# Gates by Strassen's seven products after all branch projections, and w_out opened by three token tiles

## The chip, the cores and the metric

The kernel runs on one core of one Trainium2 chip, in one launch. Its time is the device time of that core in microseconds, median of the runs given. The engines: PE (TensorE: matmuls and transposes, with PEld for its weight loads), ACT (ScalarE), DVE (VectorE), POOL (GpSimd), and SP, whose queue issues most DMAs. Each engine works through its own instructions in the order of its stream; semaphores let it wait for another engine or for a DMA. PE's results go to PSUM, which has eight banks of 128 x 512 fp32 here: two for transposes ("tr"), four for products in turn ("mm"), two for sums ("acc").

## What is computed

One layer of a hybrid decoder: two attention branches (FoX and NSA), merged by gates, an output projection, and an MLP with squared ReLU. The tokens are 512 of a prompt and 64 of samples (8 sequences of 8), D = 1024. The part that is changed is the merge and what follows it:

```python
def post_mixer(x, pm, o_fox, o_nsa, lp):
    br_fox = jnp.einsum('btk,kd->btd', o_fox.reshape(b, t_len, FOX_QW), lp['w_br_fox'])
    br_nsa = jnp.einsum('btk,kd->btd', o_nsa.reshape(b, t_len, NSA_QW), lp['w_br_nsa'])
    mix = pm['g_fox'] * br_fox + pm['g_nsa'] * br_nsa
    x = x + pm['gt1'] * jnp.einsum('btd,de->bte', mix, lp['w_out'])
    h = rms_norm(x, lp['norm2_g']) * (1.0 + pm['sc2']) + pm['sh2']
    u = jax.nn.relu(jnp.einsum('btd,df->btf', h, lp['w_up']))
    return x + pm['gt2'] * jnp.einsum('btf,fd->btd', u * u, lp['w_down'])
```

The gates g_fox and g_nsa are sigmoids of 1024 columns each of h @ w_in, where h is the normalized input. Each branch projection has 512 inputs and 1024 outputs.

## The kernel before

**fp32 by three products.** A value is split into a high part, rounded by a copy on ACT (L112, to the type fp32r), and a low part, the difference, formed on DVE (L131). A product of two such pairs is three matmuls: high by high, low by high, high by low. Names end in h or H, l or L for the parts. The tokens are worked in two halves of HALF = 288 columns, so one product of 128 output features, 1024 inputs and one half is 8 x 3 = 24 matmuls of 128 x 288.

**The mix** (`mix_part`, L1873 on) works by tiles e = 0 to 7 of 128 output features, called tiles of the mix here. For each tile and each of the two gates x it runs the gate's product (names mg, weights wm from w_in, 2 halves x 24 = 48 matmuls) and then the branch's projection (names br, weights wb, 512 inputs, 2 x 12 = 24 matmuls). ACT forms the tanh of half the gate's product out of PSUM, two instructions per gate. DVE forms (t + 1) times the branch out of PSUM (L109), which gives twice the gated branch; the factor of two is taken out later. GpSimd adds the two gated branches (L1944), and `split_pack` writes the high and low part of the sum to `mix2`, in the order that w_out's matmuls read. Tile 0 is special: its first gate is started earlier (`mix_first`), and its two branches come after both gates. The raw weights go through `praw`, a pool of three buffers of 512 KB each, filled by SP's queue.

**w_out** (`out_part`, L1980) works by token tiles i, five of them (0 to 3 of the prompt, 4 with the samples), in the order 0, 4, 1, 2, 3, and for each by q = 0 to 3: q % 2 is the half of the inputs, q // 2 the half of the 1024 outputs. So (i, q) is 12 matmuls of 128 x 512 for tile 0 to 3, 8 for tile 4. Each q has a weight of its own, wo0 to wo3. After an odd q, DVE multiplies by the gate (`wot`) and adds to x (`x2` in the code; all of x is loaded early). A finished tile is normalized: ACT sums its squares, DVE makes the reciprocal root in small steps and scales the rows (`nsq`), and PE transposes them (names nt) to give h3, the input of the MLP. Where these transposes stand is set by hand:

```python
        rest, turn_at = {}, {(1, 1): 0, (2, 0): 4, (2, 3): 1}
```

This reads: ahead of the matmuls of (1, 1) come the transposes of tile 0, ahead of (2, 0) those of tile 4, ahead of (2, 3) those of tile 1; those of tile 2 come after the last matmul. `self.chain` fixes the order of PE in this stage to that of the code; the other engines' order comes from a scheduler that places instructions by its own model.

**up** (`mlp_up`) is the MLP's first projection. Most of its tiles are already formed by Strassen's seven products, from pairs of feature tiles and the two halves of tokens and inputs, by `product`, with sums of the weights made on DVE at first and on GpSimd later (L2116).

## Time and profile before

| | us |
|---|---|
| median of 3 runs | 1194.47 |
| lowest and highest run | 1192.92, 1195.43 |
| the profiled run, by the clock of the runs | 1193.61 |
| its span in the profile | 1191.8 |

The span is the time from the first to the last instruction of the profiled execution. All positions in the text are microseconds from its start. In a row of the timeline the numbers are the start and the duration; then come the engine, the line, the operation, out<-in, and in brackets the idle time ahead of it and what ended it. In a group there stand the count, the busy time, the mean of one in ns, and the idle time ahead.

### The profile page before, as it was taken

To read this page: it belongs to the slowest core of one execution; us is meant where nothing else is said; L and a number is where in the kernel's file an instruction comes from. 1 tells how busy PE (TensorE), PEld (TensorE's weight loads), DVE (VectorE), ACT (ScalarE), POOL (GpSimd) and SP (SyncE) were. 2 spreads that over 40 slices of the span, in tenths; PEclk is the share of its full clock that TensorE was granted. 3 is DMA by queue.
4 is the path that set the end of the run, shared out by engine and by line. 5 is a ranking of instruction groups with operands and counts; after the bars stand their busy time and mean duration, and the time that the engine had idled before them with its cause. 6 is when DMAs were issued, how large, how long until landed. Compare 5 with 4: busy or idle time off the path is not lost.

```text
span 1191.8 us, 24394 instructions
## 1 busy us (share of the span) xinstructions
PE 1149.2 (96%) x9111; PEld 986.7 (83%) x9111; DVE 767.8 (64%) x1968; ACT 558.7 (47%) x1185; POOL 159.6 (13%) x174
## 2 busy tenths in 40 slices
PE   3899999999999999999999999999999999999998
PEld 3887789999666656777799999789999997888886
DVE  3588785586788866666643434668767844554586
ACT  2455463353777864555532223356556656222230
POOL 2012100000321130000300000002565400000000
PEclk9999999999999989999999999999999999999999
DMA  9599555796685457999963333355534535445312
GB/s 211 158 248 260 168 147 194 248 321 225 189 287 175 136 165 248 324 298 308 230 171 85 79 95 122 103 176 180 162 133 163 186 133 191 153 173 166 111 28 80
DMA packets 166840, 215.35 MB, mean 181 GB/s; under 512 B 18329, under 2 KB 136546, under 8 KB 164546
## 3 DMA queue, kind: packets, MB, share of 16 engines
q1 hardware_dynamic: 145602, 174.21, 47.5%
q0 software_dynamic: 9280, 25.16, 6.8%
q10 hardware_dynamic: 11840, 14.42, 3.9%
q8 instruction: 72, 1.18, 0.4%
q14 instruction: 46, 0.38, 0.1%
HBM read 190.11 MB, written 44.53 MB: 197 GB/s over the span
## 4 chain that ended last, share of the span: by engine, by line
PE 81%; DVE 6%; DMA 5%; ACT 3%; SPq 3%; issue 2%; ACTq 0%; DVEq 0%
PE dn L77 17%; PE mg L77 9%; PE z L77 6%; PE hid L77 5%; PE br L77 4%; PE wo L77 4%; PE up L77 3%; SPq L162 3%; PE ss L77 3%; PE so L77 2%; PE k L83 2%; PE ct L83 2%; DMA cpg<-in_cache_nsa_kv 2%; PE ada L77 1%; PE sp L83 1%
## 5 line engine op out<-in xcount | busy, mean ns | idle before, releaser
L77 PE MATMUL z<-winh,h 128*128 128x264 f32 (+1 forms) x576 | 111.0, 286 | 0.3
L77 PEld LDWEIGHTS z<-winh,h 128*128 128x128 f32 x576 | 91.7, 190 | 2.1 <-DVE h L794 0.9
L77 PE MATMUL z<-winl,h 128*128 128x264 f32 (+1 forms) x320 | 88.2, 284 | 0.5 <-DVE winl L131 0.5
L112 ACT ACTIVATE xh<-ct 128x256 fp32r<-128x256 f32 x128 | 48.0, 384 | 61.6 <-PE ct L83 36.0
L77 PE MATMUL mg<-hH,wml 128*128 128x288 f32 x256 | 75.4, 296 | 0.9 <-DVE wml L131 0.9
L77 PE MATMUL mg<-hH,wmh 128*128 128x288 f32 x256 | 75.4, 296 | 0.0
L100 DVE TENSOR_TENSOR acc<-acc,dn 128x512 f32<-128x512 f32 x60 | 41.0, 684 | 51.0 <-PE dn L77 50.9
L77 PE MATMUL mg<-hL,wmh 128*128 128x288 f32 x256 | 72.6, 294 | 0.0
L131 DVE TENSOR_TENSOR xl<-ct,xh 128x256 fp32r<-128x256 f32 x128 | 51.6, 420 | 16.0 <-ACT xh L112 14.2
L77 PEld LDWEIGHTS z<-winl,h 128*128 128x128 f32 x320 | 60.6, 190 | 0.7 <-DVE winl L131 0.7
L83 PE MATMUL ct<-identF,ro 128*128 128x128 f32 x256 | 36.5, 283 | 23.0 <-DVE ro L115 22.8
L131 DVE TENSOR_TENSOR wml<-wmr,wmh 128x1024 fp32r<-128x1024 f32 x14 | 17.1, 1225 | 56.4 <-ACT wmh L112 56.4
L83 PEld LDWEIGHTS ct<-identF,ro 128*128 128x128 f32 x256 | 30.2, 147 | 25.8 <-DVE ro L115 18.5
L77 PEld LDWEIGHTS mg<-hH,wml 128*128 128x128 f32 x256 | 48.1, 188 | 1.1 <-DVE wml L131 1.1
L77 PEld LDWEIGHTS mg<-hH,wmh 128*128 128x128 f32 x256 | 48.1, 188 | 0.2
L77 PEld LDWEIGHTS mg<-hL,wmh 128*128 128x128 f32 x256 | 47.2, 188 | 0.1
L77 PE MATMUL hid<-xh,w1hlv 128*128 128x512 f32 (+1 forms) x160 | 44.7, 365 | 0.7 <-ACT xh L112 0.5
L77 PE MATMUL hid<-xh,w1hlk 128*128 128x512 f32 (+1 forms) x160 | 44.6, 367 | 0.1
L131 DVE TENSOR_TENSOR wp<-sums,wp 128x1024 fp32r<-128x1024 f32 x26 | 38.0, 1468 | 9.2 <-ACT wp L112 8.5
L112 ACT ACTIVATE mgt<-mg 128x288 f32<-128x288 f32 x32 | 12.9, 410 | 59.1 <-PE mg L77 59.1
L131 DVE TENSOR_TENSOR wp<-pu,wp 128x512 fp32r<-128x512 f32 (+1 forms) x26 | 30.2, 1167 | 14.7 <-ACT wp L112 14.7
L77 PE MATMUL br<-oH,wbh 128*128 128x288 f32 x128 | 37.8, 296 | 0.2 <-ACT mgt L112 0.2
(1163 smaller groups left out, 3572.7 us busy)
## 6 DMA issues: line engine op xcount, KB each, us to landing
adw<-in_w_ada SPq DMA_DIRECT2D x16, 1024.0 KB
foxD<-in_cache_fox_kv SPq DMA_DIRECT2D x128, 128.0 KB
wdr<-in_w_down SPq DMA_DIRECT2D x32, 512.0 KB
cpg<-in_cache_nsa_kv SPq DMA_DIRECT2D x120, 128.0 KB
fr<-foxD SPq DMA_DIRECT2D x28, 512.0 KB
sr<-in_cache_nsa_kv SPq DMA_DIRECT2D x112, 128.0 KB
pu<-in_w_up SPq DMA_DIRECT2D x26, 512.0 KB
uD<-u ACTq DMA_DIRECT2D x16, 576.0 KB
```

Source lines behind the costliest of these rows:

```text
L77: ins = self.nc.tensor.matmul(out, a, b, start=start, stop=stop, skip_group_check=True)
L83: ins = self.nc.tensor.transpose(out, in_, self.identF[:n, :n])
L100: self.nc.vector.tensor_tensor(out, a, b, op=op)
L112: return self.nc.scalar.activation(out, in_, f, **kw)
L131: self.splits.append((eng or self.nc.vector).tensor_tensor(l, x, h.bitcast(F32), op=OP.subtract).ins)
L162: self.issued[eng] = getattr(self.nc, eng).dma_start(out, in_).ins
```

## The change

**The branches first.** Tile 0's two gates run as before. Then come all 16 branch projections, n = 0 to 15 (x = n // 8, e = n % 8). Those of tile 0 are gated at once by DVE as before; the other 14 are copied out of PSUM by ACT into fp32 tiles `br` (two copies each), which share their place with the later `mix` tiles. Weights of branches are split three branches ahead.

**The gates of tiles 1 to 7 by seven products.** The two gates of a tile are the two feature blocks of a Strassen scheme, the two halves of the tokens and the two halves of the inputs the others. Each of seven products has 12 matmuls (4 x 3), so a tile has 84 where it had 96. Needed for it: four differences T1 to T4 of blocks of h, formed once by DVE during the branches (1152 columns each) and split; and per tile four sums s1 to s4 of blocks of the two gates' weights, formed by GpSimd (512 columns each), and splits of seven weight blocks. The raw weights of a tile are two halves (gp_0, gp_1), each with both gates' columns for 512 inputs. Three banks A, B, E take the products; ACT copies A after the first product, and DVE adds the banks up. The last two products of a tile (`left`) run inside the next tile. Tanh, multiplication and sum are now 1152, 1152 and 576 wide, once per tile.

**w_out.** It opens with q = 0 for tiles 0, 4, 1, then q = 1 for them; the transposes move accordingly; wo2 and wo3 change their raw buffers. The place of x holds the sums (`gsums`) until the gates are done, so the loads of x come late, behind those of wo0 to wo2.

The core of the diff:

```diff
+    def gate_weights(self, x, raw, pin=None, eng=None):
+
+        t = self.pqr.tile([P, 2, D], F32R, tag="s12", bufs=2, name=f"wm{x}")
+        return self.stream(None, self.cols(self.I["w_in"], TOK + D * x, P), [P, NK, P], "wm", f"{x}", raws=0, parts=1,
+                           room=[t[:, c].rearrange("p (k f) -> p k f", k=NK) for c in range(2)], raw_at=raw, pin=pin, eng=eng)
...
+    def gate_pair_load(self, e):
+
+        self.gpr = [self.praw.tile([P, 4, 256], F32, tag="raw", bufs=3, name=f"gp{e}_{a}") for a in range(2)]
+        for a in range(2):
+            for x in range(2):
+                c = TOK + D * x + P * e
+                self.dma("sync", self.gpr[a][:, :, P * x:P * x + P],
+                         self.I["w_in"][0, 512 * a:512 * a + 512, c:c + P].rearrange("(k p) c -> p k c", p=P))
+
+    def gate_pair(self, pq, e, sums):
+
+        r1, r2 = self.gpr
+        s1, s2, s3, s4 = [sums[:, 512 * i:512 * i + 512].rearrange("p (k f) -> p k f", k=4) for i in range(4)]
+        a11, a21, a12, a22 = [r[:, :, P * i:P * i + P] for r in (r1, r2) for i in range(2)]
+        for out, a, b, op in ((s1, a21, a22, OP.add), (s2, s1, a11, OP.subtract), (s3, a11, a21, OP.subtract),
+                              (s4, a12, s2, OP.subtract)):
+            self.nc.gpsimd.tensor_tensor(out, a, b, op=op)
+        four = lambda t, c=0: t[:, :, c:c + 512].rearrange("p e (k f) -> p e k f", k=4)
+        w11 = four(pq.tile([P, 2, 512], F32R, tag="w11", bufs=2, name=f"g11{e}"))
+        w12 = self.pqr.tile([P, 2, D], F32R, tag="s12", bufs=2, name=f"g12{e}")
+        wr = (self.pw0.tile([P, 2, D], F32R, tag="w0", bufs=2, name=f"gr{e}") if e < NK - 1 else
+              self.pqr.tile([P, 2, D], F32R, tag="s12", bufs=2, name=f"gr{e}"))
+        wr = wr.rearrange("p e (k f) -> p e k f", k=4)
+        t3, t4 = [four(pq.tile([P, 2, 512], F32R, tag=f"s{n}", name=f"gs{n}{e}")) for n in (3, 4)]
+        self.split(w11[:, 0], w11[:, 1], a11)
+        self.split(wr[:, 0], wr[:, 1], r2)
+        self.split(w12[:, 0], w12[:, 1], sums[:, 0:1024])
+        self.split(t3[:, 0], t3[:, 1], s3)
+        self.split(t4[:, 0], t4[:, 1], s4)
+        return [(t[:, 0], t[:, 1]) for t in (w11, wr[:, :, :, 0:P], wr[:, :, :, P:256], four(w12), four(w12, 512), t3, t4)]
+
+    def product(self, pb, w, x, first):
+        n = 0
+        for k in range(4):
+            for a, b in three(w, x):
+                self.mm(pb[:, 0:HALF], a[:, k, :], b[:, k, :], first and n == 0, n == 11)
+                n += 1
...
+        jobs = {3: lambda: difference(1, block(rm[:, 0:1152]), b[0][1], b[0][0]),
+                4: lambda: difference(2, flat(us("t2")), b[1][1], temp[1]),
+                8: lambda: (turned(2, 0), turned(1, 0)),
+                10: lambda: difference(4, temp[2], b[1][0], temp[2]),
+                11: lambda: difference(3, flat(us("t3")), b[1][1], b[0][1]),
+                12: lambda: self.gate_pair_load(1)}
+        ws = {}
+
+        def ready(e):
+            ws[e] = self.gate_pair(pq, e, rm[:, 2048 * (e % 2):2048 * (e % 2) + 2048])
+            if e + 1 < NK:
+                self.gate_pair_load(e + 1)
+
+        for n in range(2 * NK):
+            x, e = n // NK, n % NK
+            if n in jobs:
+                jobs[n]()
+            if n + 3 < 2 * NK:
+                wb[n + 3] = branch_weights(n + 3)
+            if n == 2 * NK - 2:
+                ready(1)
+            w = wb.pop(n)
+            for hf in range(2):
+                pb = self.mmb(f"br{n}{hf}")
+                for k in range(4):
+                    for c, (a, h) in enumerate(three(w, o[x])):
+                        self.mm(pb[:, 0:HALF], a[:, k, :], tokens(h, k, hf), k + c == 0, k == 3 and c == 2)
+                s = slice(HALF * hf, HALF * hf + HALF)
+                if e == 0:
+                    self.stt(u0[:, x, s], u0[:, x, s], 1.0, pb[:, 0:HALF], OP.add, OP.mult)
+                else:
+                    if e not in br:
+                        br[e] = pm.tile([P, 2, NT], F32, tag=f"m{e}", name=f"br{e}")
+                    self.act(br[e][:, x, s], pb[:, 0:HALF])
+            if n == NK:
+                self.tt(u0[:, 0], u0[:, 0], u0[:, 1], OP.add)
+                mix2.append(pm.tile([P, 2 * NT], F32R, tag="m0", name="mix0"))
+                self.split_pack(mix2[0], u0[:, 0])
+        turned(3, 1)
+        turned(4, 1)
+
+        (b11, _), (b21, b22) = b
+        left = None
+        for n in range(1, NK + 1):
+            if n < NK:
+                if n + 1 < NK:
+                    ready(n + 1)
+                else:
+                    self.wo0 = self.out_weights(0)
+                w11, w12, w22, s1, s2, s3, s4 = ws.pop(n)
+                A, B, E = self.accb(f"mg{n}a"), self.mmb(f"mg{n}b"), self.mmb(f"mg{n}e")
+                a, bb, e = [t[:, 0:HALF] for t in (A, B, E)]
+                x = rm[:, 4096 + HALF * (n % 2):4096 + HALF * (n % 2) + HALF]
+                u = us(n)
+                q = [[u[:, g, HALF * t:HALF * t + HALF] for t in range(2)] for g in range(2)]
+                self.product(A, w11, b11, True)
+                self.act(x, a)
+                self.product(B, s2, T[2], True)
+                self.tt(q[0][1], bb, x, OP.add)
+            if left:
+                left()
+            if n == NK:
+                break
+            self.product(E, s1, T[1], True)
+            self.product(A, w12, b21, False)
+            self.act(q[0][0], a)
+            self.product(B, s3, T[3], False)
+            self.tt(q[1][1], bb, x, OP.add)
+            self.tt(q[1][1], e, q[1][1], OP.add)
+
+            def left(n=n, w22=w22, s4=s4, B=B, E=E, bb=bb, e=e, x=x, u=u, q=q):
+                v = br[n]
+
+                def gated(t0, t1, eng):
+                    s = slice(t0, t1)
+                    self.act(u[:, :, s], u[:, :, s], AF.Tanh, scale=0.5)
+                    self.stt(u[:, :, s], u[:, :, s], 1.0, v[:, :, s], OP.add, OP.mult)
+                    eng.tensor_tensor(u[:, 0, s], u[:, 0, s], u[:, 1, s], op=OP.add)
+
+                self.product(B, w22, T[4], False)
+                self.tt(q[1][0], bb, x, OP.add)
+                if n == NK - 1:
+                    gated(0, HALF, nc.vector)
+                self.product(E, s4, b22, False)
+                self.tt(q[0][1], e, q[0][1], OP.add)
+                if n == NK - 1:
+                    gated(HALF, NT, nc.vector)
+                else:
+                    gated(0, NT, nc.gpsimd)
+                mix2.append(pm.tile([P, 2 * NT], F32R, tag=f"m{n}", name=f"mix{n}"))
+                for t0, t1 in ((0, HALF), (HALF, NT)) if n == NK - 1 else ((0, NT),):
+                    self.split_pack(mix2[n], u[:, 0], None, t0, t1)
+        self.chain = None
...
-        ws = [self.wo0, self.out_weights(1), self.out_weights(2, pw)]
-        ws += [self.out_weights(3, pin=(self.splits[-1], self.last_high))]
+        ws = [self.wo0, self.out_weights(1), self.out_weights(2)]
+        pin = self.splits[-1], self.last_high
+
+        def x_load(i):
+            with self.tc.issue_after(self.loaded):
+                self.loaded = nc.sync.dma_start(x2[:TILES[i][1], i], self.x_rows(i)).ins
+
+        for i in (0, 4, 1):
+            x_load(i)
+        ws += [self.out_weights(3, pw, pin=pin, after=self.loaded)]
+        for i in (2, 3):
+            x_load(i)
         self.shift = self.mod_coef(1)
         g = None
         self.chain = ""
 
-        rest, turn_at = {}, {(1, 1): 0, (2, 0): 4, (2, 3): 1}
-        for i in (0, 4, 1, 2, 3):
+        rest, turn_at = {}, {(2, 0): 0, (2, 3): 4, (3, 1): 1}
+        pbs = {}
+        order = [(i, q) for q in range(2) for i in (0, 4, 1)] + [(i, q) for q in (2, 3) for i in (0, 4)]
+        order += [(1, 2), (1, 3)] + [(i, q) for i in (2, 3) for q in range(4)]
...
-        for i, (t0, m) in enumerate(TILES):
-            nc.sync.dma_start(x2[:m, i], self.x_rows(i))
```

Three places in the instructions' order, as built. First DVE at the start of the branches. ol are the low parts of the attention outputs (the branches' inputs), wb3 and wb4 low halves of weights, gsums the first and mut2 the second difference, br00 and br01 the two halves of branch 0 in PSUM:

```order
L131 TENSOR_TENSOR ol1_9241<-oT_4453,oh1_9240 128x576 x4
L131 TENSOR_TENSOR wb3_9366<-wbr3_0_9367,wb3_9366 128x512
L100 TENSOR_TENSOR gsums_9295<-hH_8748 128x1152
L100 TENSOR_TENSOR gsums_9295<-gsums_9295,hL2_9236 128x1152 x2
L100 TENSOR_TENSOR mut2_9508<-hH_8748,gsums_9295 128x1152
L100 TENSOR_TENSOR mut2_9508<-mut2_9508,hL2_9236 128x1152
L109 SCALAR_TENSOR_TENSOR mu0_9237<-mu0_9237,br00_9372 128x288
L109 SCALAR_TENSOR_TENSOR mu0_9237<-mu0_9237,br01_9386 128x288
L131 TENSOR_TENSOR wb4_9400<-wbr4_0_9401,wb4_9400 128x512
```

The five differences, of which none was there before, stand between the low parts and the two multiplications that empty branch 0's banks.

Second, ACT at the change from branches to gates (some rows between are left out; the number after g11, g12, gs3, gs4 and gr is the tile's). g12 is the high half of the first two sums of a tile, gr that of its second raw half, gs3 and gs4 those of its third and fourth sum; br5 and br7 are the copies of the branches 13 and 15; the last row is the first copy out of bank A of tile 1:

```order
L112 ACTIVATE g121_9877<-gsums_9295 128x1024
L112 ACTIVATE br5_9565<-br130_9844 128x288
L112 ACTIVATE br5_9565<-br131_9858 128x288
...
L112 ACTIVATE gr2_9965<-gp2_1_9892 128x1024
L112 ACTIVATE gs31_9879<-gsums_9295 128x512
...
L112 ACTIVATE g122_9964<-gsums_9295 128x1024
L112 ACTIVATE T3_9953<-mut3_9766 128x1152
L112 ACTIVATE gs41_9880<-gsums_9295 128x512
...
L112 ACTIVATE T4_9956<-mut2_9508 128x1152
L112 ACTIVATE gsums_9295<-mg1a_9984 128x288
```

The first sums' high half of tile 1 stands ahead of branch 13's copies, and that of tile 2 ahead of T3, T4 and tile 1's first copy.

Third, DVE at the end of w_out. The tile of each row can be told by the number: wot3_3 is the last product (tile 3, q = 3), nsq2 the scaled rows of tile 2, wu the low halves of up's first weights. Before:

```order
L131 TENSOR_TENSOR wu1l_11376<-wur0_0_11383,wu1h_11375 128x1024
L109 SCALAR_TENSOR_TENSOR nrs1_2_11228<-ntt151_11231,nrs1_2_11228 128x1
L131 TENSOR_TENSOR wu1l_11376<-wur1_0_11387,wu1h_11375 128x1024
L104 TENSOR_SCALAR nsq2_11225<-x2_10779,nrs1_2_11228 128x1024
L131 TENSOR_TENSOR wu2l_11378<-wur2_0_11391,wu2h_11377 128x1024
L100 TENSOR_TENSOR wot3_3_11300<-wo2_3_11275,gp1_10848 128x512
L100 TENSOR_TENSOR x2_10779<-x2_10779,wot3_3_11300 128x512
L131 TENSOR_TENSOR wu2l_11378<-wur3_0_11395,wu2h_11377 128x1024
```

and now:

```order
L131 TENSOR_TENSOR wu2l_11433<-wur2_0_11446,wu2h_11432 128x1024
L100 TENSOR_TENSOR ntt151_11260<-nrs1_2_11257 128x1
L100 TENSOR_TENSOR wot3_3_11355<-wo2_3_11330,gp1_10903 128x512
L100 TENSOR_TENSOR ntt151_11260<-ntt151_11260,nth151_11259 128x1
L100 TENSOR_TENSOR x2_10834<-x2_10834,wot3_3_11355 128x512
L109 SCALAR_TENSOR_TENSOR nrs1_2_11257<-ntt151_11260,nrs1_2_11257 128x1
L131 TENSOR_TENSOR wu2l_11433<-wur3_0_11450,wu2h_11432 128x1024
L104 TENSOR_SCALAR nsq2_11254<-x2_10834,nrs1_2_11257 128x1024
```

The scale of tile 2 stood ahead of the last product, and now stands behind it, behind its addition to x and behind one low half of a weight.

More of the change, by code (lines that the diff above doesn't have):

```diff
@@ L1891, in halves @@
-        def halves(name, w, h, n, ks=None):
-            pbs = [self.mmb(f"{name}{hf}") for hf in range(2)]
-            todo = [(hf, k) for hf in range(2) for k in range(n)] if ks is None else [(hf, k) for k in range(n) for hf in range(2)]
-            for hf, k in todo:
-                for c, (a, b) in enumerate(three(w, h)):
-                    self.mm(pbs[hf][:, 0:HALF], a[:, k, :], b(k, hf), k == 0 and c == 0, k == n - 1 and c == 2)
-            return pbs
-        def hs(t, k0=0):
-            return lambda k, hf: t[:, k0 + k, HALF * hf:HALF * hf + HALF]
@@ L1903, in gate @@
-        def gate(e, x, w, ks=None):
-            t = pq.tile([P, NT], F32, tag="mgt", bufs=2, name=f"mgt{e}{x}")
-            if e + x == 0:
-                pbs = self.g0
-                for k in range(NK):
-                    for hf in range(2):
-                        self.mm(pbs[hf][:, 0:HALF], w[0][:, k, :], hs(hL)(k, hf), False, k == NK - 1)
-            else:
-                pbs = halves(f"mg{e}{x}", w, (hs(hH), hs(hL)), NK, ks)
-            for hf, pb in enumerate(pbs):
-                self.act(t[:, HALF * hf:HALF * hf + HALF], pb[:, 0:HALF], AF.Tanh, scale=0.5)
-            return t
@@ L1916, in branch @@
-        def branch(e, x, w, t):
-            for hf, pb in enumerate(halves(f"br{e}{x}", w, (hs(oH, 4 * x), hs(oL, 4 * x)), 4)):
-                v = t[:, HALF * hf:HALF * hf + HALF]
-                self.stt(v, v, 1.0, pb[:, 0:HALF], OP.add, OP.mult)
-        def weights(e, x):
-            pin = None if e else (self.last_exp,)
-            return (self.gate_weights(e, x) if e else self.gate_weights(0, 1, self.graw, pin, False) if x else self.w0,
-                    self.stream(pq, br_src(x, e), [P, 4, P], "wb", f"{x}_{e}", raws=0, parts=1, pin=pin,
-                                after=None if e else self.first))
@@ new lines, in mix_part, with difference @@
+        b = [[[t[:, 4 * a:4 * a + 4, HALF * e:HALF * e + HALF] for t in (hH, hL)] for e in range(2)] for a in range(2)]
+        block = lambda t: t.rearrange("p (k t) -> p k t", k=4)
+        f = lambda t: t.bitcast(F32)
+        T, temp = {}, {}
+        def difference(n, out, x, y):
+            self.tt(out, f(x[0]), f(y[0]) if isinstance(y, list) else y, OP.subtract)
+            self.tt(out, out, f(x[1]), OP.add)
+            if isinstance(y, list):
+                self.tt(out, out, f(y[1]), OP.subtract)
+            temp[n] = out
@@ L2144, in ready @@
                 self.pair_load(n + 1)
-        def product(pb, w, x, first):
-            n = 0
-            for k in range(4):
-                for a, b in three(w, x):
-                    self.mm(pb[:, 0:HALF], a[:, k, :], b[:, k, :], first and n == 0, n == 11)
-                    n += 1
         ready(FIRST)
@@ L2183, in left @@
             def left(n=n, w22=w22, s4=s4, B=B, E=E, b=b, e=e, x=x, u=u, o=o):
[L2184 removed]
+                self.product(B, w22, t4, False)
                 self.tt(o[1][0], b, x, OP.add)
[L2186 removed]
+                self.product(E, s4, b22, False)
                 self.tt(o[0][1], e, o[0][1], OP.add)
```

149 lines of the change are left out of this document (81 added, 68 removed).

## The prediction

> **What bounds the kernel now.** First the page: the busy shares, then the chain that ended last.
>
> ```profile
> PE 1149.2 (96%) x9111; PEld 986.7 (83%) x9111; DVE 767.8 (64%) x1968; ACT 558.7 (47%) x1185; POOL 159.6 (13%) x174
> ...
> PE 81%; DVE 6%; DMA 5%; ACT 3%; SPq 3%; issue 2%; ACTq 0%; DVEq 0%
> ```
>
> PE bounds most of the span, but that is a mean. So next the busy time by stage: the mix from its first branch on, the opening of w_out, the rest of w_out, and up's pair loop (columns: PE, PEld, DVE, ACT, POOL, clock, DMA share, GB/s).
>
> ```profile
> 597.79:737.69 139.90, 139.90 (x1056) 139.90 (x1057) 54.91 (x75) 41.04 (x68) 10.03 (x7) 1.00 0.41 109
> 737.69:751.72 14.03, 13.50 (x66) 10.25 (x65) 11.08 (x14) 7.61 (x10) 0.00 (x0) 1.00 0.49 156
> 751.72:795.36 43.64, 43.64 (x211) 35.93 (x209) 29.22 (x90) 18.28 (x39) 2.26 (x4) 1.00 0.33 98
> 834.84:977.07 142.23, 142.23 (x1070) 142.23 (x1069) 99.03 (x120) 83.67 (x109) 65.02 (x42) 1.00 0.45 152
> ```
>
> In the mix and in the rest of w_out PE has no gap, at a granted clock of 1.00: a matmul saved there is a gain, and a wait put there is a loss in full. Only the opening has a gap. The last row is the model for the new mix: up's loop already runs seven products per tile, with PE full and DVE at 99.03 of 142.23 us.
>
> **The change, part by part.** Positions are those of the profiled run (span 1191.8, time 1193.61 us), moved by the terms before them.
>
> *1. Fewer matmuls.* Seven tiles have 84 gate matmuls where they had 96: 7 x 12 = 84 fewer. One costs 139.90 / 1056 = 0.1325 us in the first window, and a product of up's loop gives the same, 1.59 / 12:
>
> ```profile
> 834.84 1.59 PE up3a L77 x12
> ```
>
> Term: 84 x 0.1325 = **-11.1**.
>
> *2. The opening of w_out.* PE waits for weights here:
>
> ```profile
> 740.42 1.04 PE L83 MATMUL gp<-identF,modT 128*128 128x128 f32 x8
> 741.21 0.48 PE L77 MATMUL wo<-wo1h,mix 128*128 128x512 f32 x1
> 742.31 0.50 PE L77 MATMUL wo<-wo1l,mix 128*128 128x512 f32 x1 [0.39 <-DVE wo1l L131]
> ```
>
> Twelve matmuls took 740.42 - 737.69 = 2.73 us, eight transposes 0.79, so the stretch's 48 and 16 need 4 x 2.73 + 2 x 0.79 = 12.5 of its 14.03. With three tiles on wo0 and then three on wo1, wo1 is due 5 us later and wo2 some 11, and the waits go: **-1.6**. The loads of x, now behind three weights, are wanted by the first x add only, some 12 us into the stage; that cover gone, each us that they are late would wait for nobody until PE lacks a bank.
>
> *3. Branch 2.* PE uses four banks in turn, so branch 2 needs those of branch 0, which DVE frees by two gated multiplies. Ahead of these now stand on DVE a low half of 512 and five differences of 1152.
>
> ```profile
> 591.39 5.43 DVE L131 TENSOR_TENSOR oL<-oT,oH 128x576 fp32r<-128x576 f32 x8
> 597.79 0.40 PE L77 MATMUL br<-oH,wbh 128*128 128x288 f32 x1 [0.17 <-ACT mgt L112]
> L100 DVE TENSOR_TENSOR R<-R 128x1152 f32<-128x1152 f32 x4 | 5.4, 1355 | 1.9 <-DMA R<-hvD 1.9
> L109 DVE SCALAR_TENSOR_TENSOR mgt<-mgt,br 128x288 f32<-128x288 f32 x32 | 14.4, 450 | 16.8 <-PE br L77 16.8
> ```
>
> DVE is free at 596.8; 0.7 and five of 1.355 end near 604.3, the first multiply near 604.75 to 605.05; PE arrives at 597.79 + 48 x 0.1325 = 604.15. Term **+0.9** (0 to 1.5).
>
> *4. From the branches to the first gate tiles.* The largest unknown. GpSimd now makes four 512-wide sums for each tile, while DVE makes low halves and differences. How the two meet today:
>
> ```profile
> 624.09 1.43 POOL L1944 TENSOR_TENSOR mgt<-mgt,mgt 128x576 f32<-128x576 f32 x1 [17.60 <-DVE mgt L109]
> 624.15 1.92 DVE L131 TENSOR_TENSOR wbl<-wbr,wbh 128x512 fp32r<-128x512 f32 x1 [0.21 <-ACT wbh L112]
> 633.77 0.69 DVE L131 TENSOR_TENSOR wbl<-wbr,wbh 128x512 fp32r<-128x512 f32 x1 [0.26 <-ACT wbh L112]
> 906.07 1.29 POOL L2116 TENSOR_TENSOR sums<-pu,pu 128x512 f32<-128x512 f32 x1 [2.85 <-DVE wp L131]
> 907.43 2.17 POOL L2116 TENSOR_TENSOR sums<-sums,pu 128x512 f32<-128x512 f32 x1
> 828.47 3.87 POOL L2116 TENSOR_TENSOR sums<-pu,pu 128x512 f32<-128x512 f32 x1 [16.93 <-DMA pu<-in_w_up]
> 829.23 1.35 DVE L131 TENSOR_TENSOR T3l<-R,T3h 128x1152 fp32r<-128x1152 f32 x1
> ```
>
> A low half takes 0.69 alone and 1.92 when a GpSimd add began just before it: it stood until the add ended. A sum takes 1.29 alone, 2.17 beside single DVE instructions, and 3.87 beside a row of them, while the 1152-wide low half kept its 1.35: there GpSimd stood. So adds and low halves share something, and a long row of DVE's keeps GpSimd out.
>
> Now the chain. The second raw half of tile 1 takes the buffer of branch 13's weight, is asked for near 633 and lands near 637, by these two rows (a load of the same size, issue to use 4.2 us):
>
> ```profile
> 791.97 0.37 SPq L188 DMA_DIRECT2D wur<-in_w_up  x1
> 796.17 1.06 ACT L112 ACTIVATE wu2h<-wur 128x1024 fp32r<-128x1024 f32 x1 [3.29 <-DMA wur<-in_w_up]
> ```
>
> Three sums of tile 1 need it. DVE then has the differences for T3, so I take one sum at 3.87 and the rest at 2.17 to 2.28, with the end of the fourth: 647.5. Only then does the buffer take tile 2's half: landed at 651.7, two sums of tile 2 at 655.8. ACT has the high half of these ahead of T3, of the fourth sum of tile 1, of T4, and of the first copy out of a gate bank. Its rows:
>
> ```profile
> L112 ACT ACTIVATE wp<-sums 128x1024 fp32r<-128x1024 f32 x26 | 27.4, 1054 | 11.0 <-DVE sums L2116 3.0 <-PE up3e L77 1.8 <-PE up6e L77 0.9
> 814.83 1.17 ACT L112 ACTIVATE T0h<-R 128x1152 fp32r<-128x1152 f32 x1 [1.92 <-DVE R L100]
> L112 ACT ACTIVATE mgt<-mg 128x288 f32<-128x288 f32 x32 | 12.9, 410 | 59.1 <-PE mg L77 59.1
> ```
>
> 655.8 + 1.05 + 1.17 + 0.6 + 0.41 + 1.17 + 0.41 = 660.6 for the end of that copy. The branches end at 597.79 + 0.9 + 384 x 0.1325 = 649.6. Before that, ACT's high half of tile 1's first two sums stands ahead of the drains of branch 13, whose banks branch 15 needs at 646.4: +1.2. PE wants to accumulate into the copied bank after three products, at 650.8 + 3 x 1.6 = 655.6: +4.9. A third wait, w22 of tile 1 behind a DVE add that stands after tile 3's sums: 0 to 2, taken as 1. Term **+7.1**. Lower bound: sums at 1.29 save about 7 us of the chain and leave 0.5; upper: two more sums at 3.87 add 3.3 and w22's wait 1 more: 11. I take the middle rows because DVE then has both single instructions and rows of them.
>
> The steady loop I cost at nothing: per tile DVE's two-input work of about 6.1 us (0.69 for 512, 1.23 for 1024, less the overlap of ends) and GpSimd's 4 x 1.29 + 1.43 = 6.6 make 12.7, less some 0.1 for each of a dozen overlaps, against 84 x 0.1325 = 11.1 on PE. It is close; if it doesn't fit, rival B has the price.
>
> *5. The norms between w_out's tiles.* Transposes of a tile's scaled rows stand at fixed places on PE; the scale stands on DVE.
>
> ```profile
> 793.07 0.75 DVE L104 TENSOR_SCALAR nsq<-x,nrs 128x1024 f32<-128x1024 f32 x1
> 794.57 1.03 PE L83 MATMUL nt<-identF,nsq 128*128 128x128 f32 x8
> 794.87 0.68 DVE L100 TENSOR_TENSOR wot<-wo,gp 128x512 f32<-128x512 f32 x1
> 795.59 0.69 DVE L100 TENSOR_TENSOR x<-x,wot 128x512 f32<-128x512 f32 x1
> 797.26 1.23 DVE L131 TENSOR_TENSOR wu2l<-wur,wu2h 128x1024 fp32r<-128x1024 f32 x1 [0.98 <-ACT wu2h L112]
> ...
> 754.38 0.16 DVE L100 TENSOR_TENSOR ntt<-nti 128x1 f32<-128x1 f32 x1
> ```
>
> Tile 0: its scale stands behind the product of (1, 3), which PE has only just ended when it comes to the transposes: 0.68 + 0.75 = **+1.4**. Tile 1: behind (2, 3) come product, x add, seven small steps at a pace of 0.19 and the scale, 0.68 + 0.69 + 1.3 + 0.75 = 3.4 to 3.8, and PE has (3, 0) with 2.73 for it: **+0.9** (0.6 to 1.1). Tile 2: today the scale (793.07) ends ahead of the last product (794.87). In the new order it stands behind the last product, its x add and a low half of wu2, whose raw load took 4.2 us from issue above and can't be issued until a split behind the norm of tile 0 frees its buffer. Without that load 0.68 + 0.69 + 1.23 + 0.75 + 0.2 = 3.5, with it up to 6.3; DVE enters with a backlog of the other low halves, so I take **+5.8**.
>
> Sum: -11.1 - 1.6 + 0.9 + 7.1 + 1.4 + 0.9 + 5.8 = +3.4, so 1197.0 against the run's own 1193.61. The median of the three runs is 1194.47, 0.9 above it, and by that 1197.9; I say 1197.5.
>
> [...]
>
> **The rivals.**
>
> A: *the two engines take turns after every instruction.* Then a sum waits for one DVE instruction at most, so 2.2 for each but never 3.87, and the T3 differences come late instead. For it: 907.43. Against: 828.47. The chain gets 2 to 5 us shorter, term 4 falls to 2 (0.5 to 3), and the time is 1197.5 - 5.1 = 1192.4 (1189.5 to 1194.5). This is the side of faster or no change.
>
> B: *the gate loop is bound by what DVE and GpSimd share.* 12.7 against 11.1 for seven tiles is at most 11 us; two tiles of slack lie ahead and the overlaps take most, so 2 to 6 remain, on top of the forecast: 1201.5 (1199.5 to 1203.5). It decides from a pace of 11.2 us per tile on. For it: the sum. Against: up's loop, with more DVE work per tile (99.03 in 142.23), keeps PE full.
>
> C: *all waits are covered*, as in up's loop, the norms too, except for 0 to 5 us: 1194 - 12.7 = 1181 to 1187. Against: three of the waits follow from the order on one engine alone, whatever the durations.
>
> That seven products are formed where eight were follows from the program's order, so no rival leaves that out.
>
> **How the numbers follow.** Forecast 0.48 (own range 1194.5 to 1200.5), A 0.27, B 0.12, C 0.13. A measurement of this kernel tells about 0.2% from no change, 2.4 us: faster is below 1192.1, slower above 1196.9. Faster: C and 0.4 of A, 0.13 + 0.11 = 0.24. Slower: B and 0.6 of the forecast, 0.12 + 0.29 = 0.41. Same: the rest, 0.35. The range leaves out C, half of B's upper part and little else: 1188 to 1202.5.
>
> **What would show it.** Matmuls of the mix at 0.1325 each with 84 fewer (term 1); no idle of PE before wo1l, wo2l, wo3l (2); idle of about 1 us before branch 2, released by the gated multiply (3); idle near the end of the branches and before the second half of tile 1's A bank, released by ACT, and GpSimd sums of 2 to 4 us there (4); idle of 3.5 to 6 us before the transposes of tile 2 and of about 1 before those of tiles 0 and 1, released by the scale (5). PE full through tile 1 would make the forecast wrong by term 4; transposes of tile 2 without a gap, by 5.8; a pace over 11.2 us in tiles 3 to 7 would be B.

## The result, and the profile after

| | before | after |
|---|---|---|
| median of 6 runs, us | 1194.25 | 1212.86 (1207.14 to 1214.92) |
| profiled span, us | 1191.8 | 1210.4 |
| ratio, with its 95% interval | | 1.0149 (1.0131 to 1.0167) |

The change makes the kernel 1.5% slower: 18.6 us where 3.4 were forecast, outside the range. The shares of the chain that ended last, on the page of the changed kernel:

```profile
PE 72%; DVE 9%; DMA 7%; ACT 4%; SPq 3%; issue 2%; POOL 1%; ACTq 0%; DVEq 0%; POOLq 0%
```

PE had 81% before; DMA, DVE, ACT and for the first time POOL gained. The stages after (branches; gates from tile 1 to w_out's first matmul; w_out), same columns as before:

```profile
601.04:651.92 50.88, 50.88 (x386) 50.88 (x385) 29.83 (x32) 22.77 (x46) 7.54 (x5) 1.00 0.32 88
651.92:741.72 89.80, 80.28 (x566) 78.15 (x565) 74.88 (x83) 42.69 (x63) 50.00 (x30) 0.96 0.32 89
741.72:813.18 71.46, 61.90 (x298) 49.97 (x297) 47.90 (x125) 30.38 (x57) 5.46 (x8) 0.98 0.53 155
```

The branches run without a gap. In the gates and in w_out PE has gaps, and the granted clock is no longer 1.00. What PE waited for from 575 to 860 us (total, times, longest):

```profile
PE nt L83 <- DVE ntx L106: 5.6, 1, 5.6
PE mg1a L77 <- ACT gsums L112: 4.1, 1, 4.1
PE nt L83 <- DVE nsq L104: 2.2, 2, 1.4
PE mg L77 <- DMA hL<-hfd: 2.0, 4, 0.8
PE mg1b L77 <- DVE mu L100: 2.0, 1, 2.0
PE mg5b L77 <- DVE mu L100: 1.6, 1, 1.6
PE mg4b L77 <- DVE mu L100: 1.6, 1, 1.6
PE mg L77 <- DVE wm L131: 0.9, 1, 0.9
PE wo L77 <- ACT wo3h L112: 0.5, 1, 0.5
PE wo L77 <- DVE wo3l L131: 0.5, 1, 0.5
PE wo L77 <- DVE wo1l L131: 0.5, 1, 0.5
...
```

By positions of the matmuls in the two traces, the 18.6 us of span are:

| stretch | before | after | difference |
|---|---|---|---|
| up to the first gate matmul | 578.59 | 578.25 | -0.3 |
| first gate to first branch | 19.20 | 22.79 | +3.6 |
| branches and gates (24 matmuls of tile 7 that stand inside w_out counted here) | 139.90 | 143.86 | +4.0 |
| w_out, first to last matmul (less those 24) | 57.04 | 61.06 | +4.0 |
| last w_out matmul to up's pair loop | 39.95 | 47.11 | +7.2 |
| the rest | 357.1 | 357.3 | +0.2 |

In the third row the 84 matmuls less are worth -11.1; so the gates lost 15.1. By place, 8.5 of them lie between the first products of tiles 1 and 2 (16.45 us for 60 matmuls, 7.95 of PE's own work), the change from branches to gates of the prediction's term 4, and 6.6 behind.

**The start** (a stretch that the prediction left out). The changed code fixes PE's order (`self.chain = ""`) ahead of the two gates of tile 0; before, matmuls of the second gate filled the time in which the first waited for h's low part. After, with the granted clock behind it:

```profile
588.05 1.57 PE L77 MATMUL mg<-hL,wm 128*128 128x288 f32 x10
590.44 0.57 PE L77 MATMUL mg<-hL,wm 128*128 128x288 f32 x2 [0.81 <-DMA hL<-hfd]
...
593.15 0.61 PE L77 MATMUL mg<-hL,wm 128*128 128x288 f32 x1 [0.60 <-DMA hL<-hfd]
```

```profile
592.00:596.00 4.00, 3.25 (x13) 3.04 (x14) 4.00 (x8) 2.56 (x6) 0.00 (x0) 0.57 0.79 180
```

The same window before:

```profile
592.00:596.00 4.00, 4.00 (x32) 4.00 (x31) 4.00 (x7) 3.13 (x6) 0.00 (x0) 1.00 0.91 240
```

Two microseconds of waits, and then a stretch in which PE was granted about half its clock: 0.57 in this window, where the trace before has 1.00, as it has from 578.59 to 597.79 us. The same stands behind the gap of 4.1 us and behind that of 5.6 (and behind that of 2.0 at 666 us, with 0.55 from 668.57 to 671.34):

```profile
661.00:664.50 3.50, 3.23 (x12) 2.90 (x12) 3.50 (x3) 0.63 (x2) 3.42 (x2) 0.54 0.25 72
811.60:815.00 3.40, 3.40 (x17) 3.40 (x18) 2.50 (x13) 2.23 (x7) 0.00 (x0) 0.58 0.99 329
```

**The gate loop.** Tiles 5 to 7 begin 12.0, 13.3 and 13.3 us after the tile ahead of each, where PE's own work is 11.13. One turn, from the chain of waits (start, us, what):

```profile
702.57 1.13 DVE gr L131
703.70 0.38 DVE mu L100
...
704.13 3.44 DMA gp<-in_w_in
...
707.75 1.79 issue
709.54 1.88 POOL mu L2057
...
711.44 0.69 ACT mix L112
712.16 2.76 DVE mix L795 x2
...
715.84 1.13 DVE gr L131
716.97 0.38 DVE mu L100
```

This is a ring. The low half of a tile's second raw weights on DVE frees a buffer; a load follows (3.44); GpSimd's next sum waits for it (the 1.79 of "issue" is that sum); the addition of the gated branches (mu) stands behind the sum on GpSimd; ACT and DVE split its result; and DVE's next additions and low half stand behind that split. From 703.70 to 716.97 it takes 13.27 us, where PE's work is 11.13. GpSimd's sums also stretch the links of the ring: the split on DVE took 2.75 for its two pieces, and 0.83 at tile 6, when no sums run any more:

```profile
712.16 2.75 DVE L795 TENSOR_TENSOR mix<-mu,mix 128x512 fp32r<-128x512 f32 x2 [0.20 <-ACT mix L112]
743.60 0.83 DVE L795 TENSOR_TENSOR mix<-mu,mix 128x512 fp32r<-128x512 f32 x2 [0.72 <-ACT mix L112]
```

The way through the load and GpSimd is not the only long one. In the same turn DVE is busy for 12.27 of 13.27 us (third number of the row), and ahead of the split it has only 0.20 us to spare, the number in brackets above; so its own queue is nearly as long. Much of that is standing: in e4 below, where these sums are left out, DVE is busy for 8.85 us in a turn of 11.18. The turn above, then one of e4:

```profile
703.70:716.97 13.27, 11.71 (x87) 11.26 (x86) 12.27 (x14) 5.91 (x9) 8.42 (x5) 1.00 0.29 82
688.44:699.62 11.18, 11.18 (x86) 11.18 (x85) 8.85 (x14) 6.33 (x9) 2.28 (x2) 1.00 0.37 95
```

### The profile page after: what moved, and what is told of

It reads as the page before. It is cut to its first block, busy times and chain, and to the rows that moved or that the text cites. A ratio compares the mean times of both kernels' runs of the same rounds, so it can differ in the third digit from the quotient of the medians.

```text
span 1210.4 us, 24418 instructions
## 1 busy us (share of the span) xinstructions
PE 1147.6 (95%) x9027; PEld 981.5 (81%) x9027; DVE 826.5 (68%) x2021; ACT 587.5 (49%) x1233; POOL 209.8 (17%) x201
## 4 chain that ended last, share of the span: by engine, by line
PE 72%; DVE 9%; DMA 7%; ACT 4%; SPq 3%; issue 2%; POOL 1%; ACTq 0%; DVEq 0%; POOLq 0%
PE dn L77 16%; PE z L77 6%; PE hid L77 6%; PE up L77 3%; PE ss L77 3%; PE br L77 3%; SPq L162 2%; PE wo L77 2%; PE k L83 2%; PE ct L83 2%; PE so L77 2%; DMA cpg<-in_cache_nsa_kv 2%; PE ada L77 1%; PE sp L83 1%; DMA gp<-in_w_in 1%
## 5 line engine op out<-in xcount | busy, mean ns | idle before, releaser
L77 PE MATMUL br<-oh,wb 128*128 128x288 f32 x256 | 50.9, 294 | 0.0
L77 PEld LDWEIGHTS br<-oh,wb 128*128 128x128 f32 x256 | 41.1, 188 | 0.0
L131 DVE TENSOR_TENSOR wp<-pu,wp 128x512 fp32r<-128x512 f32 (+1 forms) x26 | 27.5, 1056 | 17.7 <-ACT wp L112 17.7
L112 ACT ACTIVATE u<-u 128x1152 f32<-128x1152 f32 x29 | 33.7, 1161 | 9.0 <-DVE u L100 8.3
L77 PE MATMUL br<-ol,wb 128*128 128x288 f32 x128 | 37.8, 295 | 0.0
L115 DVE COPY ro<-cpg 128x1024 f32<-128x1024 f32 x32 | 22.5, 711 | 20.1 <-DMA cpg<-in_cache_nsa_kv 17.3
L112 ACT ACTIVATE wp<-pu 128x512 fp32r<-128x512 f32 (+1 forms) x26 | 21.9, 843 | 27.4 <-PE up L77 3.8
L100 DVE TENSOR_TENSOR u<-ud,u 128x512 fp32r<-128x512 f32 (+1 forms) x56 | 22.4, 452 | 17.7 <-ACT u L112 11.4
L77 PE MATMUL ss<-kt,bdN 128*64 128x512 f32 x64 | 34.3, 618 | 0.0
L77 PE MATMUL ss<-kt,bdF 128*64 128x512 f32 x64 | 34.3, 618 | 0.0
```

Of the source, the lines that this page charges most:

```text
L77: ins = self.nc.tensor.matmul(out, a, b, start=start, stop=stop, skip_group_check=True)
L100: self.nc.vector.tensor_tensor(out, a, b, op=op)
L112: return self.nc.scalar.activation(out, in_, f, **kw)
L115: self.nc.vector.tensor_copy(out, in_)
L131: self.splits.append((eng or self.nc.vector).tensor_tensor(l, x, h.bitcast(F32), op=OP.subtract).ins)
```

## The experiments

All are edits of the changed kernel. "Gates" is the time from tile 1's first product to w_out's first matmul (PE's own work there is 564 x 0.1325 = 74.7), "last" that from w_out's last matmul to up's pair loop; positions are from each profile, medians and ratios from the timed runs. A ratio is to the kernel before as timed in the same series (its medians there: 1193.13 to 1195.24). By these intervals only e4, e8, e9 and e11 to e14 are clear of the changed kernel; what is said of the others rests on their profiles.

| kernel | first branch | gates | last | span | median | ratio (95%) |
|---|---|---|---|---|---|---|
| before | 597.79 | | 39.95 | 1191.8 | 1194.25 | |
| after | 601.04 | 89.80 | 47.11 | 1210.4 | 1212.86 | 1.0149 (1.0131 to 1.0167) |
| e1_chain | 597.40 | 90.28 | 47.36 | 1209.4 | 1211.16 | 1.0150 (1.0118 to 1.0182) |
| e2_norm | 601.02 | 89.63 | 42.63 | 1206.5 | 1208.20 | 1.0119 (1.0099 to 1.0140) |
| e3_fill | 602.06 | 89.85 | 45.77 | 1209.4 | 1209.04 | 1.0129 (1.0112 to 1.0146) |
| e4_nosums | 600.75 | 81.55 | 48.38 | 1202.6 | 1204.39 | 1.0078 (1.0057 to 1.0100) |
| e5_madd | 603.00 | 86.04 | 47.37 | 1208.2 | 1210.74 | 1.0129 (1.0104 to 1.0154) |
| e6_pin | 599.26 | 90.00 | 47.12 | 1207.9 | 1211.61 | 1.0171 (1.0139 to 1.0203) |
| e7_oldout | 601.68 | 89.55 | 39.95 | 1211.7 | 1213.63 | 1.0161 (1.0140 to 1.0182) |
| e8_all | 597.45 | 84.37 | 44.07 | 1200.2 | 1205.95 | 1.0098 (1.0075 to 1.0121) |
| e9_best | 603.06 | 86.34 | 47.47 | 1207.6 | 1203.70 | 1.0077 (1.0054 to 1.0100) |
| e10_warm | 601.85 | 90.44 | 47.05 | 1211.2 | 1213.38 | 1.0164 (1.0134 to 1.0193) |
| e11_dve | 600.84 | 78.44 | 48.08 | 1199.4 | 1199.98 | 1.0045 (1.0027 to 1.0063) |
| e12_best | 598.96 | 77.37 | 41.71 | 1193.5 | 1193.90 | 0.9996 (0.9985 to 1.0008) |
| e13_sums | 602.37 | 78.08 | 47.97 | 1200.4 | 1199.54 | 1.0053 (1.0034 to 1.0071) |
| e14_best | 599.60 | 77.92 | 41.07 | 1192.7 | 1193.48 | 0.9995 (0.9981 to 1.0009) |

**e1_chain: PE's order fixed from the branches on.**

```diff
-        self.chain = ""
         pin = (self.last_exp,)
...
+        self.chain = ""
         b = [[[t[:, 4 * a:4 * a + 4, HALF * e:HALF * e + HALF] for t in (hH, hL)] for e in range(2)] for a in range(2)]
```

> The order of PE is fixed to that of the code only from the branches on, so the second gate's matmuls may again stand between those of the first that wait for loads of h's low part. Theory: the 2.0 us of waits for these loads and the half clock behind them (0.57 granted from 592 to 596) go; the first branch starts some 3.3 to 3.6 us earlier, the whole is 3 to 4 us below the changed kernel (some 1209), unless the earlier start is given back at branch 2 (0 to 1.3). Rival: the loads are late in themselves and cost the same in any order; then nothing changes.

The first branch begins 3.6 us earlier, and the waits for hL are gone. Branch 2 then waits:

```profile
PE br L77 <- DVE mu L109: 1.0, 1, 1.0
```

The total gains only 1.0 in span, where 3 to 4 were expected; the ratio can't tell it from the change as it was. The cause of the late start is shown, but it is worth little until other waits go: the gates take 90.28, and tiles 6 and 7 again follow at 13.3 us.

**e2_norm: the last product of w_out behind the scaling of tile 2, and e3_fill: spare matmuls in the wait.**

```diff
+                with self.tc.issue_after(self.scaled) if (i, q) == (3, 3) else nullcontext():
                     self.tt(t, pb, gp[:, cs], OP.mult)
```

> On DVE the last product of w_out (tile 3, q = 3) is put behind the scaling of tile 2. Theory: the wait of 5.6 us before the transposes of tile 2 came from the order on DVE alone; the last low half of up's second weight no longer stands ahead, and some 1.5 to 2.5 us of wait remain behind the other low halves: 3 to 4 us less, and 1.5 more if the half clock behind the wait goes with it. Rival: DVE is behind with its work anyway, and the wait stays above 4 us.

```diff
+        spare = self.accb("spare")
+        for n in range(24):
+            self.mm(spare, ws[3][0][:, 0, 0:P], ws[3][0][:, 1, :], n == 0, n == 23)
         with self.tc.issue_after(self.squares):
             rest.pop(2)()
```

> 24 spare matmuls of 128 x 512 into a free bank stand on PE ahead of the transposes of tile 2, 24 x 0.2275 = 5.5 us, as long as the wait of 5.6 there. Theory A: the half clock behind the wait (0.58 granted from 811.6 to 815, some 1.4 us of loss) comes from PE having been idle; PE that works through the wait keeps its clock, and the time falls by about 1.4 us though matmuls are added. Theory B: the recorded half clock costs nothing or has another cause: the time stays or rises by what the spare matmuls overrun.

e2: the wait of 5.6 falls to 2.5, "last" by 4.5; the order on DVE was the cause. e3, the spare matmuls, the transposes behind them and the clock then:

```profile
806.16 5.60 PE L77 MATMUL spare<-wo3h 128*128 128x512 f32 x24
811.95 1.07 PE L83 MATMUL nt<-identF,nsq 128*128 128x128 f32 x8 [0.19 <-DVE ntx L106]
```

```profile
811.95:815.35 3.40, 3.40 (x27) 3.40 (x28) 2.50 (x13) 2.68 (x8) 0.00 (x0) 1.00 1.02 329
```

The transposes began no earlier, but at a clock of 1.00 in place of 0.58: "last" is 45.77 in place of 47.11, 1.3 us shorter with 24 matmuls more. (With about the same wait, 5.6 or 5.7 us, and no spare matmuls, "last" is 47.05 to 48.38 in e1, e4, e10, e11 and e13.) Theory A: here PE's idleness cost its length, and then half the clock for some 3.4 us (0.50 from 811.0 to 814.4 in the changed kernel). Half the clock came with the four short waits at the start too, 2.0 us together (0.50 from 592.6 to 596.0).

**e4_nosums, e5_madd, e13_sums, e11_dve: the gate loop.** e4 leaves the sums out from tile 3 on, e5 moves the addition of the gated branches to DVE, e13 the sums, e11 both.

```diff
 # e4
+            if e < 3:
                 self.nc.gpsimd.tensor_tensor(out, a, b, op=op)
 # e5
-                    gated(0, NT, nc.gpsimd)
+                    gated(0, NT, nc.vector)
 # e13 (e11: this and e5's)
-            self.nc.gpsimd.tensor_tensor(out, a, b, op=op)
+            self.nc.vector.tensor_tensor(out, a, b, op=op)
```

> GpSimd makes the four sums for tiles 1 and 2 only; tiles 3 to 7 use the old contents of the place (so five tiles' gates are not the reference's; the instructions on PE, ACT and DVE stay). From the first product of tile 2 to the first matmul of w_out PE's own work is 6 x 11.13 = 66.8 us; the changed kernel took 73.35. Theory L (a ring of latencies): add of bank E on DVE, tanh, product, GpSimd's add behind a sum, high part of mix, low part, next add of E, 13.3 us per tile: without sums GpSimd's add starts at once and DVE's operations are not held up; the pace falls to 11.1 to 11.5 and the stretch to 67 to 69.5 us, 4 to 6 us less in all. Rival D (DVE alone has too much work): pace stays above 12.5, the stretch above 71.

> The 576-wide addition of the two gated branches of tiles 1 to 6 is made by DVE (0.75) in place of GpSimd (1.43, up to 1.9 beside DVE). Theory L: the ring loses GpSimd's add and the wait behind a sum, 3 to 4 us of 13.3; the pace is then PE's, 11.1 to 11.6, the stretch from tile 2 to w_out 67 to 70 us in place of 73.35, 3 to 6 us less in all. Rival S (the sum of what DVE and GpSimd share binds the loop): that sum falls by only 0.7 per tile, the pace stays at 12.5 or more and the stretch above 71.

> The four sums per tile and the mix additions are all made by DVE; GpSimd makes nothing in the gate loop, so neither holds the other up, and the ring through GpSimd is gone. DVE's own work per tile rises to some 10.5 to 10.8 us by uncontended durations, against 11.13 on PE. From tile 1's first product to the first matmul of w_out the changed kernel took 89.8 us, five edits at single waits left it at 84 to 90, and PE's own work there is 74.7. Theory (the two engines hold each other up; the ring is long for that): 78 to 83 us, and the time 5 to 10 us below the changed kernel's. Rival (DVE is short of time as such, wherever sums are made): 88 or more.

> Only the four sums per tile move to DVE; the 576-wide mix additions stay on GpSimd. If the sums are what makes the ring long (they hold the addition up on GpSimd and DVE's operations beside them), tile 1's first product to w_out takes 78 to 82 us, as with both moved (78.44), and the time is 1199 to 1203. If the additions' way through GpSimd does it, 83 us or more, as with the additions alone moved (86.04), and 1204 or more.

Without sums the tiles follow at 11.2 us and the loop's waits are gone (from tile 2's first product to w_out 67.1 us against 66.8 of PE's own work): DVE's other work, without GpSimd's sums in its way, was not the bound. The time falls by 8.5, more than expected, since tile 1 gains as well (tile 2 begins 14.46 us after it in place of 16.45). With the additions moved the stretch is 69.9, as theory L had it, but two waits (1.7 and 0.5) stay, tiles 6 and 7 begin 11.9 and 13.1 us after the tile ahead, and the gates take 86.04. So rival S is not refuted, and the time fell by 2.1 by the medians where 3 to 6 were expected. DVE is full in the turn in which the pace first falls behind PE's. That turn of e5, and one of e8 (below), which has the same edit and settles at 11.9 us per tile:

```profile
703.68:715.62 11.94, 11.45 (x86) 11.21 (x85) 11.94 (x14) 4.43 (x9) 5.85 (x4) 1.00 0.44 124
699.05:710.92 11.87, 11.44 (x86) 11.20 (x85) 11.86 (x15) 6.25 (x9) 7.60 (x5) 1.00 0.34 89
```

The prediction's sum of what DVE and GpSimd share, 12.7 us per tile, and rival S's 0.7 less for these two kernels, 12.0, lie near the paces measured, 13.3 and 11.9 (e5's last step of 13.1 aside). With the sums moved the gates take 78.08, and the additions make no difference then (78.44). In e11 and e13 theory and time came as expected or better (1199.98, where 5 to 10 us less were expected, and 1199.54). What PE waits for in the gates of e13_sums:

```profile
PE mg1b L77 <- DVE mu L100: 1.2, 1, 1.2
PE mg1a L77 <- ACT gsums L112: 0.8, 1, 0.8
```

From tile 1's to tile 2's first product it is 10.5 us in place of 16.45: the waits at the change from branches to gates came from the sums on GpSimd as well. DVE makes the 24 sums of this window in 18.4 us (four groups of six), GpSimd took 40.4 for the same 24. Groups of the gates of e13_sums, then of the changed kernel:

```profile
L131 DVE TENSOR_TENSOR T<-mut,T 128x1152 fp32r<-128x1152 f32 x2 | 2.7, 1354 | 0.0
L1891 DVE TENSOR_TENSOR gsums<-gsums,gp 128x512 f32<-128x512 f32 x6 | 4.1, 686 | 0.0
```

```profile
L131 DVE TENSOR_TENSOR T<-mut,T 128x1152 fp32r<-128x1152 f32 x2 | 4.8, 2423 | 0.0
L1891 POOL TENSOR_TENSOR gsums<-gsums,gp 128x512 f32<-128x512 f32 x6 | 10.3, 1714 | 0.2
```

Two low halves of T took 2423 ns each beside GpSimd and 1354 without. Over the whole of the gates DVE was busy for 74.88 us in the changed kernel, and for less, 71.94, with the sums added to its work:

```profile
653.25:731.33 78.08, 75.96 (x567) 75.18 (x566) 71.94 (x106) 42.72 (x61) 8.32 (x6) 1.00 0.36 100
```

By these numbers some 21 us of the 74.88 were standing, an estimate: 74.88 - (71.94 - 18.4). How much of the loss was this hold-up, and how much the addition's place behind a sum that waits for a load, isn't separated: moving the sums takes both away.

**e6_pin and e10_warm: the change from branches to gates alone.** e6 puts the split of tile 2's first sums behind T3, T4 and tile 1's first copy; e10 fills the wait of 4.1 us.

```diff
 # e6
+                copied = self.act(x, a).ins
+                if n == 1:
+                    ready(2, (self.splits[-1], self.last_high, copied))
 # e10
+            if n == 1:
+                sp = self.trb("spare")
+                for m in range(30):
+                    self.mm(sp[:, 0:HALF], w11[0][:, 0, :], b11[0][:, 0, :], m == 0, m == 29)
             self.product(A, w12, b21, False)
```

> The splits of tile 2's first two sums are put behind those of T3 and T4 and behind the first copy out of bank A of tile 1. Theory: the waits of 4.1 and 2.0 us at the second half of tile 1 come from this order on ACT and DVE; the copy then ends near 658 or 659 in place of 661.1, the first wait falls to some 1 to 2 us, the second goes, and with them at least one of the two stretches of half clock (some 1.5 each): 5 to 8 us less. Rival: T3, T4 or the sums themselves are late, since GpSimd and DVE hold each other up; then the waits stay within 1.5 us of what they were.

> The changed kernel with 30 spare matmuls of 128 x 288 into a free bank (30 x 0.1325 = 4.0 us) on PE at the place where it waits 4.1 us for the first copy out of tile 1's bank. Theory A (half clock comes from idle PE): the second product runs at 1.6 us in place of 3.2, and the time from tile 1's first product to tile 2's falls from 16.45 by 1 to 2 us, though work is added. Theory B: no change, or up to 1 us more.

Both miss. In e6 the wait of 4.1 falls to 1.2, the next rises from 2.0 to 3.6, and tile 3 waits 3.2 where it had 0.3: gates 90.00. In e10 the half clock of this stretch is gone from the record, and tile 2 begins 15.68 us after tile 1, 0.8 sooner than in the changed kernel, where 1 to 2 were expected; but the next wait is 3.4, tile 3 waits 2.7, and the gates take 90.44. Each wait taken away here came back further on: the loop, not these waits, set the length of the stage.

**e7_oldout: the new mix with w_out in the old order.**

```diff
-        order = [(i, q) for q in range(2) for i in (0, 4, 1)] + [(i, q) for q in (2, 3) for i in (0, 4)]
-        order += [(1, 2), (1, 3)] + [(i, q) for i in (2, 3) for q in range(4)]
+        order = [(i, q) for i in (0, 4, 1, 2, 3) for q in range(4)]
```

> The mix of the changed kernel with w_out in the old order of tiles (0, 4, 1, 2, 3, each with q = 0 to 3) and the old places of the transposes. Theory: the waits ahead of the transposes (5.6 + 2.2 us, and some 1.5 of half clock behind them) come from the new order and go; but (0, 1) wants tile 7 of the mix at once, whose last two products, drains, tanh, product and split take some 6 to 8 us behind its last matmul, with only 3 us of other work on PE: 4 to 7 us of wait, perhaps with a stretch of half clock. In all 2 to 5 us less than the changed kernel. Rival: the opening by three tiles covers nothing: 8 to 9 us less.

"Last" is back at 39.95, so the waits of the norms belong to the new order. But the opening now waits:

```profile
PE wo L77 <- ACT wo1h L112: 4.3, 1, 4.3
PE wo L77 <- ACT wo3h L112: 3.4, 1, 3.4
```

That gives back all of it, where 2 to 5 us less were expected. The opening by three tiles does cover some 7 us; with the new mix it has to, since the splits of wo1 now come behind tile 7's drains (in the changed kernel ACT turns to wo1 at 752.41 us, straight behind the last high half of tile 7's mix), and the loads of wo2, x and wo3 behind them.

**e8_all, e9_best, e12_best, e14_best: the edits together.** e8 has e1, e2, e5 and e6. e9 adds pins for the splits of T4, of tile 2 (all but its first weight) and of up's first weights, puts the differences behind branch 0's multiplications, and the transposes of tiles 0, 4 and 1 later. e12 drops the pins of T4 and tile 2, moves the sums to DVE, keeps the differences' place and puts the transposes of tiles 0 and 4 later; e14 puts those of tile 4 back and pins three of up's first weights in place of two.

```diff
 # e14, beside e1, e2, e11
-        rest, turn_at = {}, {(2, 0): 0, (2, 3): 4, (3, 1): 1}
+        rest, turn_at = {}, {(2, 1): 0, (2, 3): 4, (3, 1): 1}
...
-        ws = [weights(q) for q in range(4)]
+        ws = [weights(q, (self.before_up,) if q else None) for q in range(4)]
...
+                with self.pinned((freed,)):
                     jobs[n]()
```

> Four edits together: order of PE fixed from the branches on, last product of w_out behind tile 2's scaling, tile 2's first sums split behind T3, T4 and tile 1's copy, mix additions on DVE. If the parts add up: 3.6 less, 1.0 back at branch 2, 4 less, 2.8 less, 4 to 5 less: some 1198 to 1200 us. If one wait only makes room for the next (the loop takes back what the change from branches to gates gives): 1203 or more.

> The four edits, with the change from branches to gates and the norms worked over: T4 and all but the first weight of tile 2 are split behind the copy and the first addition of tile 1, the five differences behind the multiplications that empty branch 0's banks, the transposes of tiles 0 and 1 stand one place later on PE, and up's first weights are split behind the scaling of tile 2. Theory (the time is PE's own work plus the waits of an order, each with its half clock): waits of 0.9 at branch 2, 5.1 at tile 1 and 4.7 at the norms fall to 3 in all, at most one stretch of half clock stays, and the profiled span falls from 1200.2 to 1189 to 1193, the time to 1190 to 1196. Rival: the waits move on into the gate loop and to up's first weights: 1199 or more.

> As the run with all sums on DVE, and with it: PE's order fixed from the branches on, the differences behind branch 0's multiplications, the transposes of tiles 0 and 4 one or two places later, w_out's last product and up's second pair of weights behind the scaling of tile 2. If the causes found are all there is: the first branch 3.6 earlier, 7 to 11 less in the gates, 4 to 6 less at the norms with their half clock: 1191 to 1198 us, about the time of the kernel before. If waits move on again: 1200 or more.

> The version that came out level with the kernel before, with the transposes of tile 4 back at their place and three of up's first four weights split behind the scaling of tile 2. Its waits ahead of transposes were 2.6 and 1.6 us; they should fall to 0.7 or less each, 2 to 3.5 us in all: 1190 to 1192, a ratio of 0.996 to 0.998 to the kernel before. Rival: the wait moves to up's first weights, and the time stays at 1193 to 1195.

e8's median of 1205.95 is about what e1, e2 and e5 took off alone (by their medians 1.7, 4.7 and 2.1 from 1212.86, which leaves 1204.4): nothing more came of having them together, and 1198 to 1200 was missed. In e9 the waits moved on, as its rival said: 5.8 us at the last products of tile 1, which wait for an addition that stands on DVE behind a low half of late sums, and 3.1 at the transposes of tile 3. e12 and e14 are level with the kernel before, e12 as expected; from e12 to e14 the waits ahead of transposes fell from 4.2 to 2.4 us, and the time did not change measurably, where 2 to 3.5 us less were expected. No version beat the kernel before.

## Why the prediction was wrong

It named slower as the likeliest, and several terms held. But the time lay 10 us above its range.

- Term 1, -11.1: right. Branches and products run at 0.1325 us per matmul.
- Term 3, +0.9: not seen, because the gates ended 3.6 us late and DVE was done by then; with that lateness undone (e1) the wait is 1.0.
- Term 4, +7.1: the place and the releasers were right, with waits of 4.1 and 2.0; the 1.2 at branch 15 did not come (no gap in the branches). One sum at 3.87 and the rest at 2.17 to 2.28 was too high: tile 1's four took 1.37 to 2.16, the slowest of the changed kernel 2.30. With the half clock behind the two waits this place lost 8.5. As a part of the sum the term did not count for itself, as e6 and e10 show.
- Term 5, +8.1: 1.45 + 0.71 + 5.63 = 7.8 measured, each at its place. Missing was half the clock behind the last of them, 1.3 (e3).
- Term 2, -1.6: the sign was wrong. w_out lost 4.0 us, of which 2.2 are waits of the first two norms; so the opening lost some 2. The prediction gave the weights time, but didn't ask what their splits stand behind (tile 7's drains).

**The step that failed** is "The steady loop I cost at nothing". The working added up what DVE and GpSimd share, 12.7 us against 11.1 on PE, and then let it go: for overlaps, for two tiles of slack, and because up's loop fits. Measured are 13.3 us per tile once the slack is used up (tiles 6 and 7), with DVE busy for 12.27. The overlaps didn't come: DVE stood, 12.27 us of busy time against 8.85 without the sums (e4). And up's loop was no model: it was said to have more DVE work per tile, but 99.03 of 142.23 us is 7.8 in 11.13, less than the gate loop's 8.85 even without sums. The 6.1 set beside it counted two-input work alone, without the additions out of PSUM. So of the rivals it is B whose mechanism came, by its own sign (a pace over 11.2 us), with a chance of 0.12. Its price of 2 to 6 is close to the 6.6 us lost behind tile 2's first product. But the loop also decided what repairs at the change from branches to gates were worth, and the two places together lost 15.1 where term 4 had 7.1. That the sums on GpSimd are the cause is shown: moved to DVE alone (e13) the gates fall by 11.7 us and the kernel by 13.3 (11.5 by the ratios). Whether one turn is better told as the ring above or as DVE filled by work and standing stays open; at this place the two ways differ by 0.2 us.

The loop alone isn't the whole miss: the forecast's 1197.5 and these 6.6 make 1204.1, and the rest, to 1212.86, is mainly the fixed order at the start, +3.6 (one line of the diff, shown by e1), the opening of w_out, and the half clock behind waits; the first and the last of these three the prediction did not have at all. Rival A, on the other side, did not come, though the traces bear out its rule more than the forecast's 3.87: no sum of the gates took over 2.30 us (rival A has 2.2), and the two pieces of DVE's split in the turn above took 2.75 us beside two sums of 1.75.

## What to carry to other kernels

When work moves to a lightly used engine, follow one whole turn of the loop: what its instruction waits for, what stands behind it on that engine, and who waits for that. Count the time in which an engine stands for the other as work. A sum that comes out above the bound (here 12.7 against 11.1) is a forecast, and should not be set to nothing because another loop fits; compare the loops by all that the engine does. Look for lines that fix an order (here one empty string), and ask what filled the waits before. And take away the cause that sets a stage's length first: until the sums were moved, repairs of single waits in the gates were given back a few microseconds later.
